# One copy and one subtraction per weight unit, and the joint tiles' low half copied by ScalarE, in the expert stage of a two-layer hybrid model

## The chip, the core and the metric

The kernel runs on one core of a Trainium2 chip. The metric is the device time of one execution in microseconds (us). The kernel before took 1473.15 us in the median of three runs (1470.57 to 1474.54).

The engines named here: TensorE (PE in the profile, its weight loads PEld), VectorE (DVE), ScalarE (ACT), GpSimd (POOL), and SyncE (SP), whose queue issues the weight transfers. Each engine takes its instructions in the order in which they stand in its queue.

## The reference

A batch of one sequence of 256 tokens, 1024 wide, goes through two layers. Layer 0 is a gated delta rule with a dense SwiGLU, layer 1 is windowed attention with a mixture of eight experts. All weights and results are float32. The part that matters here is the mixture; each expert has a hidden size of 3584:

```python
def moe_swiglu(x, w_router, w_gate, w_up, w_down):
    bsz, t, d = x.shape
    xf = x.reshape(bsz * t, d)
    logits = (xf @ w_router).astype(jnp.float32)
    top_val, top_idx = lax.top_k(logits, TOP_K)
    top_w = jax.nn.softmax(top_val, axis=-1)
    gates = jnp.einsum('nk,nke->ne', top_w, jax.nn.one_hot(top_idx, N_EXPERTS, dtype=jnp.float32))
    out = jnp.zeros_like(xf)
    for e in range(N_EXPERTS):
        h = jax.nn.silu(xf @ w_gate[e]) * (xf @ w_up[e])
        out = out + gates[:, e:e + 1].astype(xf.dtype) * (h @ w_down[e])
    return out.reshape(bsz, t, d)
```

TOP_K is 2, so an expert gets some quarter of the 256 tokens. The layer norms, the attention and the delta rule run before that, and one layer norm after it.

## The kernel before

**Weights in two parts.** TensorE works in the type fp32r, which keeps fewer bits than float32. So every weight is split: `hi` is the weight rounded to fp32r (ScalarE copies it, L154), `lo` is the rest, weight minus `hi` (VectorE subtracts, L155). Tokens are split alike. A product is then x_hi·w_hi + x_lo·w_hi + x_hi·w_lo, three matmuls.

**Units.** Weights come in units of one transfer, 128 partitions by 2048 float32 columns, 1 MB (`unit`, L140 to L156). A unit takes the next buffer of a ring of raw buffers, which SP's queue fills, and one `hi` and one `lo` buffer out of four each. A raw buffer comes free when its unit's last subtraction is done, a `hi` and a `lo` buffer when the last matmul on them is done. `quanta[0]` says in how many pieces a unit is copied and subtracted: four of 512 columns up to the third block of expert 0, then two of 1024. In the expert stage the ring has ten raw buffers; two of them are taken away for other tiles at the end of expert 6 and early in expert 7 (L1362, L1376).

**Experts.** An expert has seven blocks of 512 hidden columns. Two blocks go together, the seventh alone. A stage is a block's gate, up or down product and takes two units; an expert has 21 stages and 42 units. The loop from L1317 loads the next stage's units (L1323) ahead of this stage's matmuls. Gate goes to the PSUM banks `mm`, up to `acc`. After the up stages of a pair ScalarE applies SiLU to the gate (L1346); then the down stages of the pair before run; then follows what this text calls a hand-over (`held`, L1352 to L1358): VectorE multiplies SiLU(gate) by up (L1356), TensorE transposes the product (`turned`, L1243), ScalarE makes its `hi` (L1246) and VectorE its `lo` (L1247). An expert has four hand-overs, three of two blocks and one of one.

**Two branches.** Slots for 128 tokens are kept per expert. Where an expert has more than 64 tokens, TensorE takes the heavy branch (`heavy`, `mm3`: L170, L171, L173), 12 matmuls per unit. Where it has at most 64, it takes the light one (`mm2`, L1195), 8 matmuls per unit: a joint tile holds the `hi` of the 64 tokens in the first half of every 128 columns and their `lo` in the second, so one matmul does both token parts. The low rows are then copied (`low`, L1189) and added to the upper ones by a matmul with a folding matrix (`addlow`, L1185). The branch is TensorE's alone: ScalarE and VectorE do the same for either, joint tiles and low rows included. Expert 0 is always heavy and makes no joint tiles.

**Joint tiles.** `packed` (L1110) fills them, for the gathered tokens `xp` twice an expert (L1144), for the hidden columns `hp` once per block, seven times an expert (L1249). ScalarE copies the first half from the transposed product in PSUM (L1114), VectorE subtracts again for the second (L1115).

**Order.** The program is written stage by stage, but a scheduler orders each engine's instructions by its own costs, so where L1356, the copies and the subtractions stand relative to each other is its choice. `issue_after` (L151, L1369) holds some of them back.

Of the kernel before, what the change touches and what calls it, by code (L numbers as in the profile page):

```python
# [23 lines left out]
F32 = mybir.dt.float32  # L24
# [6 lines left out]
P = 128  # L31
# [23 lines left out]
HALF = P // 2  # L55
# [27 lines left out]
def kernel(ctx: ExitStack, tc: tile.TileContext, A, out):  # L83
    nc = tc.nc
    V, S, G, PE = nc.vector, nc.scalar, nc.gpsimd, nc.tensor
# [48 lines left out]
    quanta = [4]  # L134
# [360 lines left out]
    for tb in range(2):  # L495
        for q4 in range(2):
            p = accb()
# [25 lines left out]
    for tb in range(2):  # L523
        for q4 in range(2):
            p = accb()
# [39 lines left out]
    p = trb()  # L565
# [189 lines left out]
    with ExitStack() as fctx:  # L755
# [3 lines left out]
        hT = tuple(fp.tile([P, NF, T], F32R, name=n, bufs=1) for n in ("hTh", "hTl"))  # L759
# [237 lines left out]
    sel, gate, pos, rank = (rt.tile([P, 2, E], F32, name=n) for n in ("sel", "gate", "pos", "rank"))  # L997
# [86 lines left out]
    with ExitStack() as mctx:  # L1084
# [22 lines left out]
                        V.tensor_add(Pe[e][:, tb, :], Pe[e][:, tb, :], half[:, :P])  # L1107
            return placed

        def packed(both, p, hi):  # L1110

            v = both.rearrange("p (k l c) -> p k l c", l=2, c=HALF)
            p, hi = (t.rearrange("p (k c) -> p k c", c=P)[:, :, :HALF] for t in (p, hi))
            S.copy(v[:, :, 0], p)  # L1114
            V.tensor_sub(v[:, :, 1], p, hi.bitcast(F32))  # L1115

        def fetch(e):
            xr[e] = per.tile([P, D], F32, name="xr", tag="x0")
# [2 lines left out]
        def gather(e):  # L1121
            xg = mp.tile([P, 2, KC, P], F32R, name="xg", tag="xg")
            xp[e] = mp.tile([P, KC * P], F32R, name="xp", tag="xp") if e else None
            pg = [accb() if e == 0 else None for _ in range(2)]

            def pick(k, tb):
                PE.matmul(pg[k // 4][:, (k % 4) * P:(k % 4 + 1) * P], x[tb][:, k * P:(k + 1) * P], Pe[e][:, tb, :],
                          start=tb == 0 and k % 4 == 0, stop=tb == 1 and k % 4 == 3)

            if e == 0:  # L1130
                for k in range(KC):
                    pick(k, 0)
            for g in range(2):
                p = pg[g] if e == 0 else trb()
                for k in range(4 * g, 4 * g + 4):
                    if e == 0:
                        pick(k, 1)
                    else:
                        PE.transpose(p[:, k % 4 * P:(k % 4 + 1) * P], xr[e][:, k * P:(k + 1) * P], ident)
                hi, lo = (xg[:, n, 4 * g:4 * g + 4, :].rearrange("p a c -> p (a c)") for n in range(2))  # L1140
                S.copy(hi, p)
                V.tensor_sub(lo, p, hi.bitcast(F32))
                if e:
                    packed(xp[e][:, 512 * g:512 * (g + 1)], p, hi)  # L1144
            return xg

        xg, xp = {}, {}
# [92 lines left out]
        def turned(s, e):  # L1240
            p = trb()
            for f in range(4):
                PE.transpose(p[:, f * P:(f + 1) * P], s[:, f * P:(f + 1) * P], ident)  # L1243
            hT = mp.tile([P, 2, 512], F32R, name="hT", tag="hT")
            hp = mp.tile([P, 512], F32R, name="hp", tag="hp") if e else None
            S.copy(hT[:, 0], p)  # L1246
            V.tensor_sub(hT[:, 1], p, hT[:, 0].bitcast(F32))  # L1247
            if e:
                packed(hp, p, hT[:, 0])  # L1249
            return hT, hp  # L1250

        def keep(e):
# [57 lines left out]
        hT, held, mine, late, kept = {}, [], [], [], None  # L1310
# [6 lines left out]
        for what, e, b in stages:  # L1317
            if what != "held":
                nxt = next(nexts, None)
                if (e, b, what) == (0, 3, "gate"):  # L1320
                    quanta[0] = 2
                if nxt:
                    ready[nxt] = loads(*nxt)  # L1323
                us = ready.pop((what, e, b))
# [64 lines left out]
    with tc.If(cv > P):  # L1389
        with tc.For_i(0, E, 1) as ei, ExitStack() as octx:  # L1390
# [13 lines left out]
            for k4 in range(2):  # L1404
                p = trb()
                for kk in range(4):
                    k = 4 * k4 + kk
# [5 lines left out]
            for b in range(NB):  # L1413
                ps = []
                for n, w in enumerate((wg_, wu_)):
                    wt = op_.tile([P, KC, 512], F32, name="wt", tag="wt", bufs=2)
                    nc.sync.dma_start(wt, w[bass.ds(ei, 1)].rearrange("e (k p) n -> p (e k) n", p=P)[:, :, 512 * b:512 * (b + 1)])
                    p = mm()
# [6 lines left out]
                p = trb()  # L1425
# [63 lines left out]
```

## Time and profile before

| | |
|---|---|
| median of three runs | 1473.15 us |
| profiled execution | 1471.83 us |
| its span | 1470.1 us |
| TensorE busy | 1337.9 us (91%) |
| VectorE busy | 1202.4 us (82%) |
| ScalarE busy | 1022.4 us (70%) |
| granted TensorE clock, mean | 0.984 |
| moved over the span | 446.8 MB, 304 GB/s |

The profiled execution took 1.7 us more than its span, which runs from its first instruction to its last. A row of instructions gives engine, line, operation, what it writes and reads, the shape, the count, and behind the bar the busy time and the mean of one in ns. Behind the next bar stands how long the engine stood idle just before them and what ended that. Matmuls overlap, so a matmul's duration is longer than the time to the next one's start. A DMA share near 1 means that the sixteen transfer engines had work all the time.

### The profile page before, as it was taken

The page shows a single profiled execution, that of the slowest core. Times are in us where ns is not written, and L with a number is a line of the kernel's source. Part 1 is how long each engine was busy: PE and PEld are TensorE (multiplying, and loading weights), DVE is VectorE, ACT ScalarE, POOL GpSimd, SP SyncE. Part 2 cuts the span into 40 slices and gives each one's busy share as a digit, 9 for nine tenths or more (in the row PEclk, how much of TensorE's full clock was granted, in tenths as well). Part 3 has the DMA queues.
Part 4 walks back from the last instruction along what each step waited for, and adds up shares of the span by engine and source line. Part 5 has one row for each costly group of instructions (what it writes and reads, how often), then busy time and mean ns, then how long its engine had stood idle before and what let it go on. Part 6 is the DMA issues. An engine that isn't in the chain of part 4 may idle for free. (4 is left out here: it accounts for less than half of the span.)

```text
span 1470.1 us, 18040 instructions
## 1 busy us (share of the span) xinstructions
PE 1337.9 (91%) x6175; PEld 1041.3 (71%) x6175; DVE 1202.4 (82%) x1674; ACT 1022.4 (70%) x1519; POOL 74.5 (5%) x97
## 2 busy tenths in 40 slices
PE   7999999999998979988999999998899998888884
PEld 5888788887777868765677777765567776555552
DVE  4885965545767969899978989889998889999997
ACT  4754455443544857798887778788888778888872
POOL 4000000001000300000000000000000000001300
PEclk9999999999998989999999999999999999999997
DMA  8631587653636989999999899999999989999990
GB/s 280 199 119 59 185 287 244 227 202 84 222 115 257 381 325 371 362 392 391 390 371 365 330 353 367 354 372 378 381 391 371 367 327 385 380 377 380 418 363 30
DMA packets 145383, 446.80 MB, mean 304 GB/s; under 512 B 12704, under 2 KB 20032, under 8 KB 145264
## 3 DMA queue, kind: packets, MB, share of 16 engines
q1 hardware_dynamic: 137072, 420.64, 76.3%
q0 software_dynamic: 5280, 18.66, 3.4%
q10 hardware_dynamic: 2912, 5.90, 1.2%
q8 instruction: 76, 1.25, 0.3%
q14 instruction: 43, 0.35, 0.1%
HBM read 435.05 MB, written 15.36 MB: 306 GB/s over the span
## 5 line engine op out<-in xcount | busy, mean ns | idle before, releaser
L155 DVE TENSOR_TENSOR lo<-raw,hi 128x1024 fp32r<-128x1024 f32 (+1 forms) x928 | 930.5, 1059 | 80.2 <-ACT hi L154 76.8
L154 ACT CAST hi<-raw 128x1024 fp32r<-128x1024 f32 (+1 forms) x928 | 792.1, 927 | 147.0 <-PE acc L171 55.6
L1356 DVE TENSOR_TENSOR msg<-msg,acc 128x512 f32<-128x512 f32 x56 | 36.6, 684 | 77.1 <-ACT hi L154 38.7
L1195 PE MATMUL acc<-lo,xp 128*128 128x512 f32 x224 | 82.2, 422 | 15.8 <-DVE lo L155 14.6
L1195 PE MATMUL acc<-lo,hp 128*128 128x512 f32 x224 | 82.8, 423 | 13.9 <-DVE lo L155 12.8
L1195 PE MATMUL mm<-lo,xp 128*128 128x512 f32 x224 | 81.5, 421 | 15.3 <-DVE lo L155 14.4
L170 PE MATMUL acc<-hi,hT 128*128 128x512 f32 x224 | 89.5, 400 | 1.9 <-ACT hi L154 1.9
L171 PE MATMUL acc<-hi,hT 128*128 128x512 f32 x224 | 88.3, 394 | 0.0
L170 PE MATMUL mm<-hi,xg 128*128 128x512 f32 x224 | 87.5, 391 | 0.5 <-PEq L1179 0.5
L170 PE MATMUL acc<-hi,xg 128*128 128x512 f32 x224 | 87.9, 392 | 0.0
L171 PE MATMUL mm<-hi,xg 128*128 128x512 f32 x224 | 87.4, 390 | 0.0
L171 PE MATMUL acc<-hi,xg 128*128 128x512 f32 x224 | 87.4, 390 | 0.0
L173 PE MATMUL acc<-lo,hT 128*128 128x512 f32 x224 | 72.0, 396 | 4.1 <-DVE lo L155 4.1
L1114 ACT CAST hp<-tr 128x256 fp32r<-128x256 f32 x49 | 18.3, 374 | 81.2 <-DVE hT L1247 81.1
L1195 PE MATMUL acc<-hi,hp 128*128 128x512 f32 x224 | 71.8, 402 | 3.3 <-DVE hp L1115 3.3
L1195 PEld LDWEIGHTS acc<-lo,hp 128*128 128x128 f32 x224 | 42.5, 190 | 43.6 <-DVE lo L155 35.5
L1195 PEld LDWEIGHTS acc<-lo,xp 128*128 128x128 f32 x224 | 41.5, 191 | 44.7 <-DVE lo L155 37.9
L1195 PEld LDWEIGHTS mm<-lo,xp 128*128 128x128 f32 x224 | 41.4, 188 | 43.5 <-DVE lo L155 36.8
L1195 PE MATMUL mm<-hi,xp 128*128 128x512 f32 x224 | 68.9, 395 | 2.2 <-PEq L1179 1.5
L1195 PE MATMUL acc<-hi,xp 128*128 128x512 f32 x224 | 70.1, 400 | 0.0
L173 PE MATMUL acc<-lo,xg 128*128 128x512 f32 x224 | 68.5, 391 | 0.8 <-DVE lo L155 0.8
L173 PE MATMUL mm<-lo,xg 128*128 128x512 f32 x224 | 68.4, 391 | 0.6 <-DVE lo L155 0.6
(411 smaller groups left out, 2325.3 us busy)
## 6 DMA issues: line engine op xcount, KB each, us to landing
raw<-in_moe_w_gate_dram SPq DMA_DIRECT2D x112, 1024.0 KB, 7.0
raw<-in_moe_w_up_dram SPq DMA_DIRECT2D x112, 1024.0 KB, 7.5
raw<-in_moe_w_down_dram SPq DMA_DIRECT2D x112, 1024.0 KB, 7.4
raw<-in_a_w_in_dram SPq DMA_DIRECT2D x12, 1024.0 KB, 5.6
raw<-in_ffn_w_gate_dram SPq DMA_DIRECT2D x11, 1024.0 KB, 5.1
raw<-in_ffn_w_up_dram SPq DMA_DIRECT2D x11, 1024.0 KB, 5.1
raw<-in_ffn_w_down_dram SPq DMA_DIRECT2D x11, 1024.0 KB, 4.9
raw<-in_b_w_in_dram SPq DMA_DIRECT2D x5, 1024.0 KB, 5.0
```

Of the source, the lines that this page charges most:

```text
L154: S.copy(hi[:, c], raw[:, c])
L155: subs.append(V.tensor_sub(lo[:, c], raw[:, c], hi[:, c].bitcast(F32)))
L170: PE.matmul(ps, xh(k), wh, start=first and k == 0, stop=False)
L171: PE.matmul(ps, xl(k), wh, start=False, stop=False)
L173: PE.matmul(ps, xh(k), wl, start=False, stop=last and k == n - 1)
L1114: S.copy(v[:, :, 0], p)
L1195: PE.matmul(ps, x[:, (k0 + i % n) * P:(k0 + i % n + 1) * P], w, start=first and i == 0, stop=last and i == 2 * n - 1)
L1356: V.tensor_mul(s_, s_, pu)
```

## The change

There are three edits. `packed` gets the low part instead of the high part, and fills the second half of a joint tile with a copy on ScalarE of the low part's columns, where VectorE subtracted. The values are the same, since the low part was made by that subtraction. Both calls pass the low part. And the number of pieces per unit becomes 1 in the expert stage, except in the stages of expert 0's first two blocks, where it is 4.

```diff
-        def packed(both, p, hi):
+        def packed(both, p, lo):
 
             v = both.rearrange("p (k l c) -> p k l c", l=2, c=HALF)
-            p, hi = (t.rearrange("p (k c) -> p k c", c=P)[:, :, :HALF] for t in (p, hi))
+            p, lo = (t.rearrange("p (k c) -> p k c", c=P)[:, :, :HALF] for t in (p, lo))
             S.copy(v[:, :, 0], p)
-            V.tensor_sub(v[:, :, 1], p, hi.bitcast(F32))
+            S.copy(v[:, :, 1], lo.bitcast(F32))
...
-                    packed(xp[e][:, 512 * g:512 * (g + 1)], p, hi)
+                    packed(xp[e][:, 512 * g:512 * (g + 1)], p, lo)
...
-                packed(hp, p, hT[:, 0])
+                packed(hp, p, hT[:, 1])
...
             if what != "held":
                 nxt = next(nexts, None)
-                if (e, b, what) == (0, 3, "gate"):
-                    quanta[0] = 2
+                quanta[0] = 1 if e or b > 1 else 4
                 if nxt:
                     ready[nxt] = loads(*nxt)
```

The scheduler then orders the queues anew. Lines after L1319 have a number lower by one in the changed kernel, so L1356 is L1355 there.

VectorE's queue around the second hand-over of an expert from the third on, before. `lo<-raw,hi` is a unit's subtraction, `msg<-msg,acc` the product of gate and up, `hT<-tr,hT` the low part of its transpose, `hp<-tr,hT` the second half of the joint tile; a branch row marks where TensorE's branch stands in the program.

```order
L155 TENSOR_TENSOR lo<-raw,hi 128x1024 x2
L1179 UNCONDITIONAL_BRANCH
L155 TENSOR_TENSOR lo<-raw,hi 128x1024 x4
L1179 UNCONDITIONAL_BRANCH x2
L1356 TENSOR_TENSOR msg<-msg,acc 128x512 x2
L155 TENSOR_TENSOR lo<-raw,hi 128x1024 x5
L1179 UNCONDITIONAL_BRANCH
L155 TENSOR_TENSOR lo<-raw,hi 128x1024
L1247 TENSOR_TENSOR hT<-tr,hT 128x512
L155 TENSOR_TENSOR lo<-raw,hi 128x1024 x2
L1115 TENSOR_TENSOR hp<-tr,hT 128x4x64
```

The same place on VectorE in the changed kernel:

```order
L155 TENSOR_TENSOR lo<-raw,hi 128x2048 x2
L1179 UNCONDITIONAL_BRANCH
L155 TENSOR_TENSOR lo<-raw,hi 128x2048 x2
L1179 UNCONDITIONAL_BRANCH
L155 TENSOR_TENSOR lo<-raw,hi 128x2048
L1179 UNCONDITIONAL_BRANCH
L1355 TENSOR_TENSOR msg<-msg,acc 128x512 x2
L155 TENSOR_TENSOR lo<-raw,hi 128x2048
L1179 UNCONDITIONAL_BRANCH
L155 TENSOR_TENSOR lo<-raw,hi 128x2048
L1247 TENSOR_TENSOR hT<-tr,hT 128x512
```

Before, the product follows the last two branch marks at once, and three whole units (six halves) stand between it and the low part of the transpose. After, one whole unit stands between those two marks, ahead of the product, and two stand between the product and the low part. All four hand-overs of experts 2 to 6 are moved so, by one unit.

ScalarE's queue behind the same hand-over, before. `hi<-raw` is a unit's copy, `hT<-tr` the high part of the transpose, `hp<-tr` the first half of the joint tile.

```order
L1246 CAST hT<-tr 128x512
L154 CAST hi<-raw 128x1024 x2
L1179 UNCONDITIONAL_BRANCH
L154 CAST hi<-raw 128x1024 x2
L1114 CAST hp<-tr 128x4x64
L154 CAST hi<-raw 128x1024
L1179 UNCONDITIONAL_BRANCH
L154 CAST hi<-raw 128x1024
L1246 CAST hT<-tr 128x512
L154 CAST hi<-raw 128x1024 x2
L1114 CAST hp<-tr 128x4x64
```

And in the changed kernel, where `hp<-hT` is the new copy of the second half:

```order
L1246 CAST hT<-tr 128x512
L154 CAST hi<-raw 128x2048
L1114 CAST hp<-tr 128x4x64
L1115 CAST hp<-hT 128x4x64
L154 CAST hi<-raw 128x2048
L1179 UNCONDITIONAL_BRANCH
L1246 CAST hT<-tr 128x512
L154 CAST hi<-raw 128x2048
L1114 CAST hp<-tr 128x4x64
L1115 CAST hp<-hT 128x4x64
```

The first half's copy now comes one whole unit behind the high part, where it came two behind, and the second half follows it directly. On TensorE the transposes of the next expert's gathered tokens (L1139) are moved forward: half of them now stand between the two gate stages of the second pair, where all stood behind both. Up to the expert stage no queue has changed.

## Rows read from the trace of the kernel before

**Rows 1.** Busy time in stretches, one per expert (0 to 7), cut where ScalarE starts on an expert's first unit. Columns: the stretch, its length, then busy us and count of PE, PEld, DVE, ACT and POOL, the granted clock, the share of the transfer engines, GB/s.

```profile
443.00:597.60 154.60, 141.26 (x656) 118.55 (x655) 126.14 (x197) 101.29 (x143) 19.46 (x20) 0.92 0.89 336
597.60:713.50 115.90, 100.94 (x417) 71.80 (x415) 107.59 (x109) 100.38 (x129) 1.07 (x2) 1.00 1.00 385
713.50:839.30 125.80, 119.70 (x532) 96.16 (x533) 108.60 (x110) 100.31 (x128) 1.07 (x2) 1.00 0.94 360
839.30:966.80 127.50, 121.31 (x542) 97.60 (x540) 108.73 (x111) 100.52 (x129) 1.06 (x2) 1.00 0.92 355
966.80:1083.70 116.90, 100.27 (x398) 67.92 (x396) 108.25 (x111) 100.16 (x129) 1.07 (x2) 1.00 0.99 386
1083.70:1209.50 125.80, 119.70 (x532) 96.11 (x532) 108.62 (x110) 100.33 (x128) 1.07 (x2) 1.00 0.94 360
1209.50:1327.30 117.80, 100.55 (x396) 67.53 (x394) 109.18 (x110) 100.22 (x129) 7.70 (x5) 1.00 1.00 379
1327.30:1441.00 113.70, 96.43 (x372) 65.28 (x373) 108.25 (x114) 96.53 (x123) 17.65 (x7) 0.98 0.92 364
```

**Rows 2.** Waits in expert 4 (966.8 to 1083.7 us). Columns: engine, what and line, what ended the wait; total us, how many, the longest.

```profile
ACT hp L1114 <- DVE hT L1247: 12.3, 7, 2.9
...
DVE msg L1356 <- PE acc L1185: 8.6, 4, 3.2
...
ACT msg L1346 <- PE mm L1185: 1.8, 2, 1.1
...
ACT hT L1246 <- PE tr L1243: 1.4, 3, 1.0
```

**Rows 3.** Timeline of VectorE around the third hand-over of expert 4. Columns: start, us taken together, engine, line, operation, tiles, count, and the idle time before with what ended it.

```profile
1037.01 13.71 DVE L155 TENSOR_TENSOR lo<-raw,hi 128x1024 fp32r<-128x1024 f32 x12
1052.53 1.29 DVE L1356 TENSOR_TENSOR msg<-msg,acc 128x512 f32<-128x512 f32 x2 [1.82 <-PE acc L1185]
1053.74 6.90 DVE L155 TENSOR_TENSOR lo<-raw,hi 128x1024 fp32r<-128x1024 f32 x6
```

**Rows 4.** Timeline of TensorE at the same hand-over, the same columns.

```profile
1050.77 0.50 PE L1195 MATMUL acc<-lo,hp 128*128 128x512 f32 x1 [0.17 <-DVE lo L155]
...
1052.03 0.62 PE L1185 MATMUL acc<-low,fold 128*128 128x512 f32 x2
1053.28 1.26 PE L1243 MATMUL tr<-ident,msg 128*128 128x128 f32 x8 [0.62 <-DVE msg L1356]
```

**Rows 5.** Timeline of ScalarE at the same hand-over, the same columns.

```profile
1039.54 7.70 ACT L154 CAST hi<-raw 128x1024 fp32r<-128x1024 f32 x8
1047.92 0.60 ACT L1346 ACTIVATE msg<-mm 128x512 f32<-128x512 f32 x1 [0.67 <-PE mm L1185]
...
1049.83 3.92 ACT L154 CAST hi<-raw 128x1024 fp32r<-128x1024 f32 x4
...
1061.27 0.37 ACT L1114 CAST hp<-tr 128x256 fp32r<-128x256 f32 x1 [2.92 <-DVE hT L1247]
```

**Rows 6.** Waits from 540 to 1440 us, all those that a DMA ended.

```profile
POOL y L1366 <- DMA raw<-in_moe_w_up_dram: 75.8, 1, 75.8
...
POOL yt L1282 <- DMA ys<-yt: 8.5, 1, 8.5
...
POOL y L1367 <- DMA y<-x3d: 5.3, 1, 5.3
...
POOL yt L1282 <- DMA raw<-in_moe_w_down_dram: 0.3, 1, 0.3
```

**Rows 7.** The page's part on transfers: the up weights, KB each, median us from issue to landing.

```profile
raw<-in_moe_w_up_dram SPq DMA_DIRECT2D x112, 1024.0 KB, 7.5
```

**Rows 8.** Busy time in three stretches, the columns of rows 1.

```profile
1190.00:1330.00 140.00, 120.76 (x483) 83.28 (x482) 127.92 (x129) 117.17 (x149) 7.70 (x5) 1.00 0.98 373
1330.00:1425.00 95.00, 81.71 (x319) 55.02 (x319) 89.55 (x90) 83.33 (x106) 16.70 (x7) 1.00 1.02 405
...
1365.00:1415.00 50.00, 43.34 (x173) 29.30 (x172) 46.36 (x46) 44.83 (x56) 12.85 (x2) 1.00 1.03 417
```

**Rows 9.** Groups of instructions by line and shape. Columns: as in the section above: count, busy us, mean ns, idle us before them and what ended it.

```profile
L155 DVE TENSOR_TENSOR lo<-raw,hi 128x1024 fp32r<-128x1024 f32 x648 | 751.5, 1220 | 9.2 <-ACT hi L154 8.8
L154 ACT CAST hi<-raw 128x1024 fp32r<-128x1024 f32 x648 | 636.7, 1060 | 23.8 <-PE acc L171 13.3 <-PE mm L171 5.5 <-ACT hi L154 2.7
L155 DVE TENSOR_TENSOR lo<-raw,hi 128x512 fp32r<-128x512 f32 x280 | 179.1, 687 | 71.0 <-ACT hi L154 68.0 <-PE mm L173 2.8
...
L1246 ACT CAST hT<-tr 128x512 fp32r<-128x512 f32 x56 | 33.1, 591 | 22.0 <-PE tr L1243 22.0
...
L1115 DVE TENSOR_TENSOR hp<-tr,hT 128x256 fp32r<-128x256 f32 x49 | 20.5, 417 | 0.0
...
L1114 ACT CAST hp<-tr 128x256 fp32r<-128x256 f32 x49 | 18.3, 374 | 81.2 <-DVE hT L1247 81.1
```

**Rows 10.** Waits in expert 2 (713.5 to 839.3 us), the columns of rows 2.

```profile
DVE msg L1356 <- ACT hi L154: 12.3, 3, 5.2
...
PE tr L1243 <- DVE msg L1356: 3.8, 4, 0.9
...
DVE msg L1356 <- PEq L1179: 3.5, 1, 3.5
...
PE acc L173 <- DVE lo L155: 1.8, 4, 0.5
```

## The prediction

> **What bounds the kernel now.** I read the page first, then the table of stretches, the operations by shape, the timelines of three engines around one hand-over, the waits of two experts, and the transfers. The code that changes runs in the expert stage, so I cut that stage into its eight experts [rows 1]. The reader is to see two kinds. Experts 2, 3 and 5 issue some 530 matmuls each and TensorE is busy for 95% of them (119.7 of 125.8 us): they run the three-matmul branch, as expert 0 does, and TensorE bounds them. Experts 1, 4, 6 and 7 issue 370 to 420 and TensorE is far less full (100.3 of 116.9 us in expert 4): they run the two-matmul branch. There VectorE has 108.25 us of work in 116.9, so 8.65 us idle, and ScalarE 100.2. VectorE bounds them, and the waits say where its idle time lies: 8.6 us in four waits of L1356, the product of gate and up, for TensorE's L1185 [rows 2].
>
> The timelines show one such wait. VectorE runs twelve subtractions in a row, the last ends at 1050.72, and then L1356 stands at the head of its queue for 1.82 us [rows 3]. TensorE in that time finishes the matmuls that needed the last subtraction, adds the low rows (L1185), and transposes once L1356 has delivered [rows 4]. VectorE's queue is in order, so no later subtraction can be taken in that gap, though ScalarE was already two copies of the next units further on [rows 5].
>
> The transfers are not the bound today: between 540 and 1440 us the only waits that a DMA ended are four of POOL's [rows 6]. But they are close. Ten raw buffers at 116.9/42 = 2.78 us per unit give 27.8 us from one issue to the next into the same buffer; 7.5 us of it is the transfer [rows 7], some 6 us the copy and the subtraction, so about 14 us is reserve. And the rate is near the highest that rows show, 417 GB/s at a share of 1.03 [rows 8], which is 1.049 MB / 417 = 2.51 us per unit.
>
> **Part 1: one copy and one subtraction per unit.** A 1024-column subtraction takes 1.220 us and a 512-column one 0.687 [rows 9], so 512 columns more cost 0.533, and one of 2048 should take 1.220 + 2 x 0.533 = 2.29 us. In a row, instructions start closer together than they last: twelve took 13.71, so (13.71 - 1.22) / 11 = 1.135 from start to start [rows 3], 0.085 less than one lasts. A unit thus costs 2.27 now and 2.29 - 0.085 = 2.20 after: 0.07 saved, 2.9 us over an expert's 42 units. No row has a 2048-column subtraction. From below, 2.13 (no fixed part at all); from above 2.44 (twice 1.220, no gain and the overlap lost). I take 2.20, the line through the two rows of the same form.
>
> The Trainium skill weighs in here: VectorE: DVE Perf Modes, section "The DRAIN you can't avoid", says that the next operation does not start before the pipeline has emptied. Taken strictly, whole durations would count, 2.44 against 2.29. By that rule 0.15 us a unit and not 0.07 would go; the starts 1.135 apart speak against it.
>
> On ScalarE a 1024-column copy takes 1.060 us, eight in a row 7.70, so 0.95 from start to start [rows 5, 9]. 256 columns more cost 0.591 - 0.374 = 0.217 [rows 9], so 2048 take 1.060 + 4 x 0.217 = 1.93, or 1.82 start to start against 1.90 for two: 0.08 a unit, 3.4 us an expert. Bounds 1.74 and 2.12, by the same reasoning.
>
> **Part 2: the low half of the joint tiles.** VectorE loses nine subtractions an expert (seven for hp, two for xp), each 0.417 us [rows 9], 0.33 start to start: 3.0 us. ScalarE gains nine copies of 256 columns from SBUF. No row has that; the same shape from PSUM takes 0.374 and 512 columns take 0.591. I take 0.39, 0.28 start to start, since the shape weighs more than the source: 2.5 us. No new wait comes with it: the copy before it (L1114) already waits for the VectorE operation that writes the low half [rows 2].
>
> **Part 3: the order moves.** This is the larger term. The order of VectorE shows L1356 one unit later: in a steady expert one more whole subtraction stands before it. The 1.82 us gap then holds 2.20 us of work that is needed next anyway. Of the four waits, 8.6 us, all but the longest (3.2) vanish, and that one keeps about 1.0. L1356 itself comes up to 0.4 us later, and TensorE pays for that with time it has to spare here (16.6 us idle in expert 4).
>
> **The sum.** VectorE in expert 4: 108.25 - 2.9 - 3.0 = 102.4, plus 1.0 of the long wait, plus what it waits for ScalarE after each joint tile: two small copies and a whole one, 0.37 + 0.39 + 1.93 less three overlaps of 0.11 = 2.36, against 2.20 of work in hand, 0.16 x 7 = 1.1. That is 104.5. ScalarE: 100.2 - 3.4 + 2.5 = 99.3, plus 1.8 it waits before L1346 [rows 2], 1.4 before the copies of the transposes [rows 2], and a wait of some 0.5 at each of seven joint tiles (it copies a unit in 1.93 while VectorE must finish one in 2.20 and the 0.6 us low half): 3.5. That is 106.0, and the later of the two counts. Expert 4: 116.9 - 106.0 = 10.9 us; expert 1: 115.9 - 106.0 = 9.9.
>
> Experts 6 and 7 follow each other, and the transfers limit them, as the ring loses two buffers there too. From 1190 to 1330 us they ran at 373 GB/s, from 1330 to 1425 at 405 [rows 8]. At 417 throughout: 140 x (1 - 373/417) + 95 x (1 - 405/417) = 14.8 + 2.7 = 17.5 us. At 405 throughout: 11.1. I take 15.
>
> Experts 2, 3 and 5: four waits of TensorE for the subtraction after each hand-over, 1.8 us an expert [rows 10], go, since that subtraction is now made ahead; VectorE idled 12.3 + 3.5 us at L1356 there, enough to take it. 5.4 us in all. The rest is TensorE's own work; neither part 1 nor part 2 is felt there, and if that cover were gone, they would save rather than cost. Expert 0: nothing. Before 443 us the order of every engine is the same: nothing.
>
> 9.9 + 10.9 + 15 + 5.4 = 41 us. The profiled execution took 1471.83 us, its span 1470.1 and 1.7 around it; 1471.8 - 41 = 1431, and the median of the runs shown lies 1.3 higher: 1432 us.
>
> **Rivals.**
> - *The gap only changes its place.* VectorE takes the early subtraction, but waits just as long elsewhere, for ScalarE's copies, which now come in pieces of 1.93 us. For it: VectorE's waits for those copies are already long where pieces are small and ScalarE is not ahead (68 us before 512-column subtractions [rows 9]). Against: 8.8 us only in 648 of 1024. Left are 5.9 us in each of four experts, 23.6: 1450 us.
> - *ScalarE becomes the bound.* It keeps all its 16.7 us of waiting per light expert: 99.3 + 16.7 = 116.0, 0.9 less than now, and TensorE's experts gain nothing: 1473 - 3.6 = 1469.5 us, no change. For it: 12.3 us of those waits are for VectorE's low half, 2.9 at the longest [rows 2]. Against: these arise because ScalarE is ahead (it stood idle with two units copied [rows 5]).
> - *Slower: lockstep at the joint tiles.* L1114 waits behind VectorE's low half, which stands behind a subtraction of 2.20 rather than 1.14, and all later copies queue behind L1114. If each of nine joint tiles adds that 1.06 us to ScalarE's kept waits, a light expert takes 116.0 + 9.5 = 125.5, 8.6 more than now; four of them make 34: 1507 us. It decides once ScalarE's waits pass 116.9 - 99.3 = 17.6 us an expert. Against: the wait shrinks as ScalarE's lead does.
> - *Whole durations count.* VectorE pays each instruction's full length, so a merged pair saves 0.15. That is 3.5 us more in experts 1 and 4 and, with the transfers giving their 17.5, 10 in all: 1422 us. The rule of the Trainium skill quoted above (VectorE: DVE Perf Modes, "The DRAIN you can't avoid") would bring this; the starts of [rows 3] contradict it.
>
> **Chances.** The forecast 0.62, its own range 1418 to 1446. The gap moved 0.17; ScalarE the bound 0.08; lockstep 0.07; whole durations 0.06. A difference under 0.3% (4.4 us) cannot be told from none. Faster: 0.62 + 0.17 + 0.06 = 0.85; same 0.08; slower 0.07. The range takes in forecast, whole durations and the moved gap, with 10 us beyond the latter for a 2048-column subtraction dearer than 2.29 (at 2.44, 0.24 x 42 = 10 us in each light expert, half of it hidden where ScalarE or the transfers pace): 1412 to 1460.
>
> **What would show it.** Right: experts 1 and 4 near 106 us, with VectorE busy 102; L155 of 2048 columns at 2.29 us and L154 at 1.93; waits of L1356 for L1185 below 3 us an expert; the transfers at 410 GB/s or more from 1200 us on, and perhaps first waits of L154 for raw; experts 2, 3 and 5 at 124. Wrong: light experts still above 112; ScalarE's waits for hT grown beyond 12 us; a wait of TensorE before L1243 grown above 1 us in the heavy experts; or ScalarE waiting for transfers already in expert 4.

## The result, and the profile after

The changed kernel takes 1425.92 us in the median of four runs (1422.09 to 1427.08), against 1471.86 for the kernel before, measured beside it: a ratio of 0.968 (95% interval 0.966 to 0.971), 46 us saved. The forecast was 1432, the range 1412 to 1460. The profiled execution took 1427.08 us, its span 1425.4, at a mean granted clock of 0.982 (0.984 before).

The busy times on the page, after:

```profile
PE 1314.1 (92%) x6175; PEld 1046.2 (73%) x6175; DVE 1165.6 (82%) x1293; ACT 1012.1 (71%) x1264; POOL 68.0 (5%) x97
```

The groups by line and shape, after; columns as in [rows 9]:

```profile
L155 DVE TENSOR_TENSOR lo<-raw,hi 128x2048 fp32r<-128x2048 f32 x322 | 726.4, 2290 | 46.6 <-ACT hi L154 39.8 <-DMA raw<-in_moe_w_gate_dram 5.9
L154 ACT CAST hi<-raw 128x2048 fp32r<-128x2048 f32 x322 | 608.5, 1929 | 30.9 <-PE acc L171 18.1 <-PE mm L171 6.6 <-PE acc L173 4.6
...
L1355 DVE TENSOR_TENSOR msg<-msg,acc 128x512 f32<-128x512 f32 x56 | 36.4, 681 | 36.5 <-PEq L1179 33.3 <-PE acc L1185 2.7 <-PE acc L173 0.5
...
L1115 ACT CAST hp<-hT 128x256 fp32r<-128x256 f32 x49 | 20.6, 420 | 0.0
L1114 ACT CAST hp<-tr 128x256 fp32r<-128x256 f32 x49 | 18.6, 380 | 54.7 <-DVE hT L1247 54.7
```

A subtraction of 2048 columns takes 2.290 us and a copy 1.929, as forecast. The product now waits only 2.7 us for L1185 over the whole run; ScalarE waits 54.7 us for the low part of the transposes, where it waited 81.2 [rows 9]. But VectorE waits 39.8 us for ScalarE's copies, in 322 instructions, where it was 8.8 in 648.

VectorE at the third hand-over of expert 4, after (start, us together, the instructions, and the idle time before):

```profile
1022.50 15.50 DVE L155 TENSOR_TENSOR lo<-raw,hi 128x2048 fp32r<-128x2048 f32 x7 [0.35 <-ACT hi L154]
1037.92 1.28 DVE L1355 TENSOR_TENSOR msg<-msg,acc 128x512 f32<-128x512 f32 x2
1039.12 4.48 DVE L155 TENSOR_TENSOR lo<-raw,hi 128x2048 fp32r<-128x2048 f32 x2
```

Seven units stand in a row where there were six, and the product follows with no wait: the 1.82 us of [rows 3] are gone at this hand-over. From start to start a subtraction takes (15.50 - 2.29)/6 = 2.20 us.

For the rest I cut the time at TensorE's last hand-over transposes (L1243) of each expert, the same place in every kernel. The stretches of experts 1 to 7 after; columns as in [rows 1]:

```profile
604.70:706.10 101.40, 87.84 (x364) 63.88 (x362) 92.77 (x55) 91.19 (x89) 1.07 (x2) 0.98 1.01 390
706.10:827.10 121.00, 116.90 (x527) 95.34 (x527) 103.96 (x59) 100.83 (x95) 1.06 (x2) 1.00 1.00 388
827.10:951.40 124.30, 119.99 (x541) 97.95 (x541) 103.90 (x59) 99.85 (x94) 1.06 (x2) 1.00 0.97 364
951.40:1059.60 108.20, 96.00 (x402) 70.17 (x402) 103.14 (x59) 97.27 (x94) 1.06 (x2) 1.00 1.01 404
1059.60:1180.60 121.00, 116.86 (x527) 95.34 (x527) 103.96 (x59) 100.91 (x95) 1.07 (x2) 1.00 1.00 387
1180.60:1288.90 108.30, 95.89 (x403) 70.19 (x403) 103.20 (x59) 97.28 (x94) 1.59 (x3) 1.00 1.01 399
1288.90:1397.30 108.40, 95.14 (x381) 68.53 (x381) 106.77 (x67) 95.79 (x89) 16.39 (x9) 0.97 1.00 406
```

The same cuts in the kernels of this study, in us, each from its own trace (whole_again and after_again repeat whole_only and the changed kernel, and agree with them within 0.3 us in every expert from the first on):

| expert | before | after | whole_only | late_product | late_joint | early_whole | joint_double | pool_low |
|---|---|---|---|---|---|---|---|---|
| up to the end of 0 | 604.2 | 604.7 | 601.9 | 606.4 | 603.4 | 601.8 | 603.0 | 601.9 |
| 1, light | 102.0 | 101.4 | 101.1 | 101.3 | 100.7 | 101.1 | 104.7 | 99.7 |
| 2, heavy | 125.9 | 121.0 | 121.0 | 122.2 | 121.5 | 124.2 | 121.0 | 121.1 |
| 3, heavy | 127.4 | 124.3 | 124.3 | 124.2 | 123.7 | 128.6 | 124.4 | 124.5 |
| 4, light | 116.9 | 108.2 | 107.0 | 109.2 | 108.0 | 115.7 | 111.2 | 105.8 |
| 5, heavy | 125.8 | 121.0 | 121.0 | 122.2 | 123.2 | 126.0 | 121.0 | 121.0 |
| 6, light | 116.9 | 108.3 | 107.0 | 109.2 | 108.0 | 115.7 | 111.2 | 105.8 |
| 7, light | 119.1 | 108.4 | 108.3 | 111.9 | 110.3 | 116.9 | 110.9 | 107.8 |
| behind it | 31.8 | 28.1 | 29.7 | 30.9 | 28.3 | 33.6 | 28.2 | 31.5 |

Of the 44.7 us between the two spans, 8.7, 8.6 and 10.7 lie in experts 4, 6 and 7, 12.8 in the heavy ones, 3.7 behind the last hand-over, 0.6 in expert 1 and -0.5 before it. The cut at the start of expert 1 lies 6.6 us behind that of [rows 1] and the one at its end 7.3 us ahead, so its stretch is shorter here; by the cuts of [rows 1] it gained 2.3 us (see below).

### The profile page after: what moved, and what is told of

Its sections match the earlier page's. It is cut to its first block, busy times and chain, and to the rows that moved or that the text cites. A ratio compares the mean times of both kernels' runs of the same rounds, so it can differ in the third digit from the quotient of the medians.

```text
span 1425.4 us, 17392 instructions
## 1 busy us (share of the span) xinstructions
PE 1314.1 (92%) x6175; PEld 1046.2 (73%) x6175; DVE 1165.6 (82%) x1293; ACT 1012.1 (71%) x1264; POOL 68.0 (5%) x97
## 5 line engine op out<-in xcount | busy, mean ns | idle before, releaser
L155 DVE TENSOR_TENSOR lo<-raw,hi 128x2048 fp32r<-128x2048 f32 (+1 forms) x610 | 910.3, 1532 | 119.1 <-ACT hi L154 109.2
L154 ACT CAST hi<-raw 128x2048 fp32r<-128x2048 f32 (+1 forms) x610 | 768.4, 1310 | 156.5 <-PE acc L171 61.3
L1195 PE MATMUL acc<-lo,xp 128*128 128x512 f32 x224 | 76.8, 431 | 22.3 <-DVE lo L155 20.1
L1195 PE MATMUL mm<-lo,xp 128*128 128x512 f32 x224 | 70.8, 403 | 9.6 <-DVE lo L155 9.4
L1195 PEld LDWEIGHTS acc<-lo,xp 128*128 128x128 f32 x224 | 39.6, 195 | 50.4 <-DVE lo L155 44.5
L1195 PE MATMUL acc<-lo,hp 128*128 128x512 f32 x224 | 71.5, 400 | 3.4 <-DVE lo L155 3.4
L1195 PE MATMUL acc<-hi,hp 128*128 128x512 f32 x224 | 70.8, 397 | 1.2 <-ACT hp L1115 1.2
L1195 PE MATMUL mm<-hi,xp 128*128 128x512 f32 x224 | 68.9, 394 | 2.2 <-ACT low L1189 1.5
L1195 PE MATMUL acc<-hi,xp 128*128 128x512 f32 x224 | 70.7, 403 | 0.0
L1355 DVE TENSOR_TENSOR msg<-msg,acc 128x512 f32<-128x512 f32 x56 | 36.4, 681 | 36.5 <-PEq L1179 33.3
L1195 PEld LDWEIGHTS mm<-lo,xp 128*128 128x128 f32 x224 | 40.2, 188 | 26.8 <-DVE lo L155 19.4
L1114 ACT CAST hp<-tr 128x256 fp32r<-128x256 f32 x49 | 18.6, 380 | 54.7 <-DVE hT L1247 54.7
L1243 PE MATMUL tr<-ident,msg 128*128 128x128 f32 x224 | 34.9, 284 | 22.5 <-DVE msg L1355 22.5
```

The lines of the kernel that those rows point to most:

```text
L154: S.copy(hi[:, c], raw[:, c])
L155: subs.append(V.tensor_sub(lo[:, c], raw[:, c], hi[:, c].bitcast(F32)))
L1195: PE.matmul(ps, x[:, (k0 + i % n) * P:(k0 + i % n + 1) * P], w, start=first and i == 0, stop=last and i == 2 * n - 1)
L1355: V.tensor_mul(s_, s_, pu)
```

## Experiments

The change consists of three things: whole units (fewer, longer instructions), the joint-tile edit, and a consequence, the product standing one unit later in VectorE's queue. Two theories. **Order**: the gain comes from the product's new place, where a subtraction fills the time that VectorE stood idle. **Instruction**: it comes from fewer and longer instructions, and from the work taken off VectorE.

**whole_only.** The number of pieces alone; the joint tiles stay with VectorE. The scheduler moves the product by one unit here too.

```diff
-                if (e, b, what) == (0, 3, "gate"):
-                    quanta[0] = 2
+                quanta[0] = 1 if e or b > 1 else 4
```

> Only the pieces per unit change: one copy and one subtraction of 2048 columns; the joint tiles are still subtracted by VectorE. The scheduler puts the product one unit later here too. Order theory (the gap before the product, 8.6 us per light expert, is what is won): VectorE keeps the 3.0 us of joint subtractions per light expert, so some 12 us above the full change: 1438 us, waits of the product for the low-row matmul under 3 us in expert 4. Instruction theory (fewer and cheaper VectorE instructions win it, the gap only moves): 0.07 us x 42 units x 4 experts = 12 us below before: 1460 us.

Measured: 1423.07 us, ratio 0.966 (0.965 to 0.968), faster than either theory said, and as fast as the whole change. VectorE is busy 105.3 us in expert 4, the 2.9 us less that the prediction gave to whole units.

**joint_only.** The edits of `packed` and its two calls alone, units in halves; the product stays in its old place.

> Only the joint tiles change: ScalarE copies their low half; units stay in two pieces and the product stays where it was in VectorE's queue. Order theory: only the 3.0 us of joint subtractions per light expert go, 12 us, and the 8.6 us gap stays in expert 4: 1460 us. Instruction theory: the joint subtractions carry nearly half of 5.9 us per light expert of VectorE's time, the same 12 us and perhaps as much again from ScalarE's shorter waits: 1448 to 1460 us. Slower than 1465 would mean that ScalarE pays for the copies.

Measured: 1468.24 us, ratio 0.998 (0.996 to 0.999). In expert 4 VectorE is busy for 105.7 us instead of 108.25, yet the expert takes 117.5 us: the product still waits 8.6 us for L1185. The 2.6 us of work taken off VectorE came back as 3.1 us of waits for ScalarE (1.7 before L1142, 1.4 for the copies; none before), and the heavy experts took 1.2 to 1.7 us longer. Both theories' numbers were missed; the third case of the expectation, that ScalarE pays for the copies, is the one that came.

**early_product.** The changed kernel with the product put back to its old place, by making the next unit's subtraction wait for it (`subs` lists the subtractions in program order; a dependency inside one engine only sets the order):

```diff
-                    V.tensor_mul(s_, s_, pu)
+                    prod = V.tensor_mul(s_, s_, pu)
...
+                if e:
+                    tc.add_manual_dep(subs[-2 if b == 1 else -4].ins, prod.ins.name, mybir.DependencyInfo(
+                        mybir.DependencyClass.NoSync, mybir.DependencyReason.DATA), reason="early product")
```

> Both edits, but two added dependencies keep the product where it stood before the change, ahead of the next unit's subtraction. Order theory: the gap comes back, so expert 4 takes about 5 us more than with the full change and the heavy experts 2 us more: 4 x 5 + 3 x 2 = 26 us, 1452 us. Instruction theory: the instructions are those of the full change, so 1426 to 1430 us, with waits of the product back and other waits shorter by as much.

Measured: 1470.49 us, ratio 0.999 (0.9981 to 1.0005): nothing is left of the 46 us, where the order theory had 1452. Expert 4 takes 114.8 us with VectorE busy for 103.0. The run is not clean: expert 1 also lost 7.2 us against the kernel before, in an order that neither kernel has there, and the last product of expert 7 stands one unit earlier than in either.

**late_product.** The reverse: the kernel before, with halves and joint tiles as they were, and only the product held back by one unit. The scheduler then also placed the low part of the transpose one unit later for some blocks (three of seven in expert 4):

```diff
+                with ExitStack() as held_back:
+                    if e:
+                        held_back.enter_context(tc.issue_after(subs[-3 if b == 1 else -7].ins))
                     for bb, pu, _, s_ in mine:
-                        V.tensor_mul(s_, s_, pu)
+                        prod = V.tensor_mul(s_, s_, pu)
...
+                            for n in (2, 1) if b == 1 else (6, 5):
+                                tc.add_manual_dep(subs[-n].ins, prod.ins.name, mybir.DependencyInfo(
```

> The kernel before, instructions and all, with the product held back by one unit in VectorE's queue. Order theory: the gap of 8.6 us per light expert is filled and the heavy experts gain 1.8 us each: 4 x 7 + 5 = 33 us, 1439 us. Instruction theory: VectorE's 108 us of work per light expert is unchanged and the idle time turns up elsewhere, 1465 to 1472 us.

Measured: 1438.44 us, ratio 0.978 (0.976 to 0.980). The stretch of expert 4, columns as in [rows 1]:

```profile
954.10:1063.30 109.20, 96.62 (x402) 69.98 (x402) 108.23 (x110) 99.90 (x127) 1.07 (x2) 1.00 1.02 406
```

And in the list of its waits all that VectorE's product still waits for TensorE (L1359 is the product here):

```profile
DVE msg L1359 <- PE acc L1185: 0.5, 1, 0.5
```

VectorE does exactly the work of before (108.23 us against 108.25) in 109.2 us instead of 116.9. The gap went, 7.6 of 8.6 us. That is the order theory's number, and 33 of the 46 us.

**early_whole.** The clean form of early_product: whole_only, with the product put back from expert 2 on (the same lines, with `e > 1`). It is not the product alone here either: the low part stands one unit later for four of seven blocks of expert 4.

> whole_again (whole units, joint tiles on VectorE) with one thing changed: from expert 2 on the product of gate and up stands where it stood before, one whole unit earlier on VectorE. Theory that the order carries the gain: the waits of the product for TensorE's L1185 come back (8.6 us or more in expert 4), experts 4 and 6 take about 115 instead of 107.1, expert 7 about 116 instead of 108.4, and the heavy experts 2, 3 and 5 about 4.4 each more, since TensorE's weight loads wait for subtractions again: 1423.2 + 7.9 + 7.9 + 7.6 + 13 = 1460. Theory that whole units carry it by fewer instructions: at most 1430.

Measured: 1466.64 us, ratio 0.997 (0.995 to 0.999); 6.6 more than the order theory's 1460, of which 3.9 lie behind the last hand-over. There the added dependency puts the product one unit earlier than in any kernel without it: before and after the change the last product stands at the same place. The stretch of expert 4:

```profile
955.80:1071.50 115.70, 99.51 (x402) 69.14 (x402) 105.46 (x68) 95.17 (x85) 1.07 (x2) 1.00 0.99 383
```

Its waits of VectorE's product:

```profile
DVE msg L1355 <- PE acc L1185: 7.6, 3, 3.6
...
DVE msg L1355 <- ACT hi L154: 2.1, 1, 2.1
```

VectorE's work is that of whole_only, and 9.7 us of waits for the product are back. Whole units without the order are worth 4 to 5 us.

**late_joint.** late_product with the joint-tile edit added, so that the edit is seen beside halves in the good order.

> late_product (the kernel before with the product one unit later, halves) with the joint-tile edit added, so the edit is seen beside halves in the good order. Theory that ScalarE's extra copies pace VectorE only where ScalarE copies whole units (a copy of 1.93 us must end before the subtraction starts, against 1.06): VectorE's saving of 2.2 to 3 us per light expert is felt, experts 4 and 6 at 107, the time 1430 to 1434. Theory that the extra copies cost VectorE as much as they save whatever the piece: 1437 to 1441, as late_product's 1438.4.

Measured: 1429.15 us, ratio 0.971 (0.969 to 0.973), 9 below late_product. The intervals of the two do not touch. Of the 10.5 us between the two traces 3.0 are there before expert 0's first matmul, where the kernels are the same; 1.2, 1.2 and 1.6 lie in experts 4, 6 and 7, and 2.6 behind the last hand-over. So the edit does pay beside halves, some 6 to 7 us, and in expert 4 by half of the 2.6 us of VectorE's work that it takes off there (105.60 busy).

**after_again and whole_again**, on one chip:

> The changed kernel once more, as the measure for the three kernels beside it. If the joint-tile edit saves time beside whole units (VectorE's 2.2 us less work in a light expert are felt), it is at least 4 us faster than whole_again. If VectorE waits for ScalarE's extra copies instead, it is 2 to 5 us slower, as the first two measurements apart suggest (1425.9 against 1423.1 us).

> The kernel with the number of pieces changed alone (joint tiles filled by VectorE's subtraction, as before). Theory that the joint-tile edit costs a little: 1423 us, 2 to 5 below after_again. Theory that VectorE's busy time alone counts: 1430, some 4 x 2.2 us less 2 above it being hidden, so above after_again.

Measured: 1425.28 (1422.01 to 1425.62) against 1423.22 us (1420.68 to 1424.66); ratios 0.968 (0.966 to 0.970) and 0.967 (0.965 to 0.969). The times overlap, so that the joint-tile edit beside whole units costs anything is not shown; that it saves 4 us is excluded. The traces say why. The stretch of expert 4 in whole_again:

```profile
948.30:1055.40 107.10, 95.67 (x402) 70.25 (x403) 105.41 (x68) 94.91 (x85) 1.07 (x2) 1.00 1.01 404
```

And in after_again:

```profile
949.80:1058.10 108.30, 95.91 (x403) 70.19 (x403) 103.25 (x59) 97.31 (x94) 1.06 (x2) 1.00 1.01 404
```

The edit takes 2.2 us from VectorE, and the expert is 1.2 us longer. From the list of waits of that stretch, VectorE's for the copies, in whole_again:

```profile
DVE lo L155 <- ACT hi L154: 0.3, 1, 0.3
```

And in after_again:

```profile
DVE lo L155 <- ACT hi L154: 3.6, 9, 0.7
```

Nine waits of 0.4 us on average. In the timeline of the changed kernel five of them, 0.35 or 0.36 us each, stand at the second subtraction behind a joint tile; the other four, 0.26 to 0.66, lie where the next expert's gathered tokens come in between. ScalarE's timeline shows how one of the five comes about:

```profile
1044.24 0.37 ACT L1114 CAST hp<-tr 128x256 fp32r<-128x256 f32 x1 [2.10 <-DVE hT L1247]
1044.51 0.41 ACT L1115 CAST hp<-hT 128x256 fp32r<-128x256 f32 x1
1044.81 1.91 ACT L154 CAST hi<-raw 128x2048 fp32r<-128x2048 f32 x1
```

And VectorE's:

```profile
1044.12 2.28 DVE L155 TENSOR_TENSOR lo<-raw,hi 128x2048 fp32r<-128x2048 f32 x1
1046.76 2.29 DVE L155 TENSOR_TENSOR lo<-raw,hi 128x2048 fp32r<-128x2048 f32 x1 [0.36 <-ACT hi L154]
```

ScalarE's queue is in order too. L1114 waits for VectorE's low part; once that is there, VectorE has one subtraction in hand, and ScalarE two small copies and a whole one (to 1046.72, 2.48 us) before the next can start.

**joint_double.** The changed kernel with the second small copy made twice.

```diff
             S.copy(v[:, :, 1], lo.bitcast(F32))
+            S.copy(v[:, :, 1], lo.bitcast(F32))
```

> The changed kernel, with ScalarE's copy of the low half made twice (63 more copies of 0.42 us, some 3.4 us of ScalarE per expert; VectorE's and TensorE's work unchanged). Theory that ScalarE's copies around a joint tile pace VectorE in the light experts: VectorE's waits for ScalarE's copies grow by about 0.35 us at each joint tile of a light expert, 7 to 9 of them, so 2.5 to 3 us for experts 4 and 6, and the time is 1433 to 1438 us. Theory that ScalarE has reserve there (97 of 108 us busy): at most 1 us more, 1426 to 1428.

Measured: 1437.19 us, ratio 0.977 (0.974 to 0.979), 11.9 above after_again. Experts 1, 4, 6 and 7 take 3.2, 2.9, 2.9 and 2.5 us more, the heavy ones nothing. In expert 4 ScalarE is busy for 100.5 of 111.2 us and VectorE for 103.3, and still:

```profile
DVE lo L155 <- ACT hi L154: 6.5, 10, 0.9
```

That grew by 2.9 us (3.6 before), as much as the expert. ScalarE is idle for 10.7 us there and yet sets the pace: 6.9 us of that is waiting at L1114 for the low part, and its work on the next unit queues behind.

**pool_low.** The second small copy on GpSimd.

```diff
-            S.copy(v[:, :, 1], lo.bitcast(F32))
+            G.tensor_copy(v[:, :, 1], lo.bitcast(F32))
```

> The changed kernel, with the low half copied by GpSimd, which has almost nothing to do in the expert stage, instead of ScalarE. TensorE's order is the same, row for row. If ScalarE's copy is what costs, VectorE's waits for ScalarE fall to those of whole_again, VectorE keeps its 2.2 us saving, and the time is 1416 to 1421 us. If the transfers already pace experts 6 and 7, only experts 1 and 4 gain, 1421 to 1424. Rival: GpSimd's copy takes several us, and TensorE then waits for the joint tile in the down stage: 1430 or more.

Measured: 1422.15 us (1420.72 to 1422.94), ratio 0.966 (0.965 to 0.968). TensorE's order is the changed kernel's. Experts 4 and 6 fall to 105.8 us, 2.5 below after_again, but the stretch behind the last hand-over is 3.4 us longer. TensorE waits there 2.95 us for GpSimd's last copy, which takes 2.39 us, where it waited 1.17 us for ScalarE's in the changed kernel (more on that end below). So the rival came true at one place. The time lies in the second theory's range, but not for its reason, since expert 6 gained as much as expert 4. It is the lowest median of the study, 1.1 below whole_again, which is within what such runs scatter. From 1200 us on its transfers run at the highest rate that any row here shows (stretches, columns as in [rows 1]):

```profile
1200.00:1330.00 130.00, 115.39 (x479) 82.87 (x478) 126.98 (x72) 117.33 (x106) 31.25 (x21) 1.00 1.03 416
1330.00:1380.00 50.00, 43.28 (x174) 31.35 (x174) 49.89 (x34) 43.12 (x38) 11.39 (x5) 0.95 1.03 417
```

42 units of 1.049 MB in 105.8 us are 416 GB/s too. VectorE (103.25 us busy in expert 4's 105.7) is all but full there as well, and only one wait for a transfer is in the expert stage's trace, 0.6 us on ScalarE.

**All of it in one table** (medians in us, the kernel before at 1470.6 to 1471.8 beside each; the changed kernel is the last cell; between the rows the product's place differs, from expert 2 on in the third column and from expert 1 on in the others):

| product | halves, subtraction | halves, copy | whole, subtraction | whole, copy |
|---|---|---|---|---|
| early | 1471.8 | 1468.2 | 1466.6 | 1470.5 |
| late | 1438.4 | 1429.2 | 1423.2 | 1425.3 |

The order is worth 33 to 45 us in every column; in the last column 7.8 of the 45 are expert 1's, and in both whole columns 2 to 4 us lie behind the last hand-over, where the early kernels' product stands earlier than in any other. Without it neither edit is worth more than 5.2. With it, whole units bring 15.2, the joint edit 9.3, and both together 13.1, each with an uncertainty: in the traces late_product is 2 to 3 us behind the others before expert 0's first matmul, where nothing differs. They draw on the same few us per light expert, and then ScalarE's copies are next. That the transfers are is not shown.

## Why the prediction was right, and where it was not

**Durations.** Right. 2.29 and 1.93 us were the line through the shorter shapes, and 2.20 from start to start came out to the hundredth. The rival of whole durations falls with it: seven subtractions of 2.29 took 15.50 us, not 16.03. The sentence of the Trainium skill behind it (VectorE: DVE Perf Modes, "The DRAIN you can't avoid") thus does not hold here as taken strictly; the paragraph goes on to say that an operation that is not held starts earlier, and that is what these rows show.

**The order.** Right, and now tested both ways: late_product has it without the two cheaper forms, early_whole has whole units without it. The scheduler moved some low parts too in both, so what they test is the order around the hand-over; that the product carries it is told by its own waits, gone in one and back in the other. In expert 4 the waits of the product for L1185 fell from 8.6 to 1.3 us (forecast: 1.0 left). The rival that the gap only changes its place is excluded by late_product, where time and gap went together.

**VectorE after the joint tiles.** The mechanism was right, the size was not. The sum gave 0.16 us at seven tiles, 1.1 us; measured are 3.6 us at nine. At the tile shown above ScalarE's three copies took 2.48 us where the sum had 2.36, they began 0.12 us after the subtraction in hand, and the next one started 0.04 us after the last copy's end: 0.36 us. The two xp tiles were left out. Three times as much waiting, with 3.0 us of subtractions saved that turned out 2.2 (busy, whole_again to after_again), makes the joint edit cost 1.2 us beside whole units in expert 4, where I put it at 3.0 saved per light expert. The sum's later path was ScalarE's, 106.0 us: 99.3 of work and 6.7 of waits, 3.5 of them at L1114. Measured are 97.3 of work, and 7.2 at L1114 alone. Expert 4 gained 8.7 us, not 10.9. The rival of ScalarE as the bound is thus true in part: not by its busy time, but by what stands behind L1114.

**Heavy experts.** Forecast 1.8 each, measured 4.9, 3.1 and 4.8. The step that failed is the reading of TensorE's waits: I took them from its matmuls [rows 10]. The weight loads have waits of their own. Expert 2 before, from the list of waits:

```profile
PEld tr L1243 <- DVE msg L1356: 7.3, 8, 1.4
PEld acc L173 <- DVE lo L155: 2.6, 3, 0.9
PEld acc L1195 <- DVE lo L155: 2.0, 3, 0.9
PEld mm L173 <- DVE lo L155: 0.7, 1, 0.7
```

The waits for `lo` are 5.3 us in seven, close to the 4.9 gained; 2.0 of them, the light branch's L1195, belong to the last down stage of expert 1, which this stretch takes in. Expert 5, which also follows a light expert, has 5.3 us of them too and gained 4.8; expert 3, which follows a heavy one, has 3.0 and gained 3.1. Of expert 2 after, the same list has none of them, and all of the waits before the transposes still:

```profile
PEld tr L1243 <- DVE msg L1355: 7.3, 8, 1.4
PEld acc L1185 <- ACT low L1189: 0.6, 1, 0.6
```

The wait for a `lo` tile stands at the weight load ahead of the matmul that reads it. The matmuls of that stretch show only 2.2 us of such waits; part of the lost time is hidden in their rows, whose busy time fell from 119.2 to 116.9 us with the same work. late_product leaves 0.5 us of such waits and 122.2 us; early_whole loses 3 to 5 us in each of these experts again.

**Expert 1.** The worst step: 9.9 us forecast, 2.3 measured. In the cuts of [rows 1], which the forecast went by, its 115.9 us became 113.6:

```profile
598.10:711.70 113.60, 100.04 (x419) 74.00 (x418) 104.11 (x60) 99.14 (x96) 1.07 (x2) 0.98 1.01 391
```

I treated it as expert 4. In its stretch of the table the product's 5.1 us of waits went, and VectorE has 2.1 us less work, but its waits for ScalarE's copies grew from 0.8 to 7.0 us, one of them 3.1 long. The timeline of the changed kernel has that one at the first copy after a wait of ScalarE:

```profile
624.40 1.91 ACT L154 CAST hi<-raw 128x2048 fp32r<-128x2048 f32 x1 [3.82 <-PE acc L171]
```

And on VectorE's timeline right behind it:

```profile
626.35 2.29 DVE L155 TENSOR_TENSOR lo<-raw,hi 128x2048 fp32r<-128x2048 f32 x1 [3.09 <-ACT hi L154]
```

Expert 0 is heavy, TensorE still works on its units, and ScalarE has no free `hi` buffer until it is done with one. Before, these two waits were there too, but of 2.14 and 0.50 us. VectorE does not come to this place earlier now, so the wait grew for other reasons. One is that the subtraction now needs a whole copy of 1.91 us, where half a unit's took 1.05. The other is TensorE's clock. In both kernels TensorE stands idle for some 2 us just before, and sixteen matmuls of L1195 follow. Before, the granted clock stayed at 1.00 and they took 3.8 us; now they took 5.4, since for some of it the clock was at its lower level, 1.2 GHz:

```profile
618.00:620.00 2.00, 2.00 (x6) 1.59 (x5) 2.00 (x2) 1.31 (x1) 0.00 (x0) 0.50 1.00 363
```

Why it fell in one and not in the other is open. This is read from the traces; no run changed the number of buffers, so whether a fifth would free these 3 us is open too. That ScalarE paces the rest of this expert too is shown: joint_double lost 3.2 us in it, and pool_low gained 1.8.

**Experts 6 and 7, and the end.** Forecast 15, measured 8.6 + 10.7 = 19.3, and 3.7 behind the last hand-over that I had not counted. I had let the transfers bound both experts. Expert 6 is bounded as expert 4 is, and takes the same 108.3 us. The transfers came near the highest rate of any row here, 417 GB/s, only from 1300 us on: in the changed kernel 406 GB/s from 1190 to 1300, 416 from 1300 to 1390. That they bounded even expert 7 is not shown: VectorE is busy there for 106.8 of 108.4 us, and no engine but GpSimd waits for a transfer. The 5.9 us that the row of L155 puts to one are four waits in experts 1, 2, 3 and 5. Each ends 0.03 us after a copy of ScalarE's that had run for 1.9 us, and this copy reads the same transfer, so they are waits for the copy.

The 3.7 us at the end go with the joint edit: they are there in joint_only (28.2 against 31.8), and only 2.1 of them in whole_only. The last joint tile makes them. TensorE before, after, and in pool_low, where it begins on that tile:

```profile
1446.14 0.70 PE L1195 MATMUL acc<-hi,hp 128*128 128x512 f32 x2 [3.29 <-DVE hp L1115]
```

```profile
1402.97 0.73 PE L1195 MATMUL acc<-hi,hp 128*128 128x512 f32 x2 [1.17 <-ACT hp L1115]
```

```profile
1395.01 0.73 PE L1195 MATMUL acc<-hi,hp 128*128 128x512 f32 x2 [2.95 <-POOL hp L1115]
```

VectorE filled the second half behind two subtractions (2.35 us), ScalarE fills it at once, and GpSimd's copy takes 2.39 us. After the two longer waits the granted clock was 0.57 over the next 4 us, that is for most of them at 1.2 GHz, and two matmuls there took 1.05 us; after the shorter one it stayed at 1.00 and they took 0.62.

**The sum.** 41 forecast, 44.7 in the spans. In the cuts of [rows 1], errors of -7.6 (expert 1), -2.2 (expert 4), +7.4 (heavy), +6.3 (from expert 6 on, the end taken in) and -0.5 (before expert 1) nearly cancelled. The total was closer than its steps, and that is luck. Lockstep, the slower rival, did not come: ScalarE's waits for the low part fell in all.

## What to carry to other kernels

Where an engine with an in-order queue waits at its head while its next independent work is ready, look at what stands behind that instruction before making any instruction cheaper: one product moved by one unit was worth 33 us of 1472 here, and both cheaper forms without it some 5 at most. When work is handed from a full engine to one with idle time, ask where that idle time lies: ScalarE had some 11 us of it in each light expert, most of it at the head of the copies that VectorE then waited for. And read the waits of TensorE's weight loads beside those of its matmuls, since there the wait for a late tile was 5.3 us where the matmuls showed 2.2.

## What the runs showed of the hardware

GpSimd and VectorE hinder each other. Timelines of pool_low, GpSimd's copies first:

```profile
979.82 0.40 POOL L1115 CAST hp<-hT 128x256 fp32r<-128x256 f32 x1 [25.25 <-DVE hT L1247]
...
1038.11 2.40 POOL L1115 CAST hp<-hT 128x256 fp32r<-128x256 f32 x1 [21.62 <-DVE hT L1247]
```

and VectorE's at the third hand-over of expert 4:

```profile
1037.36 0.68 DVE L1247 TENSOR_TENSOR hT<-tr,hT 128x512 fp32r<-128x512 f32 x1
1037.96 4.68 DVE L155 TENSOR_TENSOR lo<-raw,hi 128x2048 fp32r<-128x2048 f32 x2
```

The same copy takes 0.40 us where no subtraction was running when it began, and 2.40 where one had begun 0.15 us before. The two subtractions of which the first began so, with such a copy beside them, take 4.68 us, against 4.48 in the changed kernel. So the copy waits for the subtraction (2.28 us) to end, and the next subtraction pays 0.2 us for it. The Trainium skill says this (SBUF — State Buffer, "Summary: rules for kernel authors"): of a VectorE instruction with two SBUF inputs and a GpSimd instruction that reads SBUF, the second to issue blocks until the first has finished. The trace agrees. In expert 4 seven of the nine copies took 2.39 or 2.40 us, so pool_low still pays up to 1.4 us for it there. Where VectorE had begun an instruction that reads PSUM, the trace shows the copy undisturbed. GpSimd first:

```profile
985.61 0.40 POOL L1115 CAST hp<-hT 128x256 fp32r<-128x256 f32 x1 [1.67 <-DVE hT L1247]
```

and VectorE, with `tr` in PSUM:

```profile
985.45 0.68 DVE L1142 TENSOR_TENSOR xg<-tr,xg 128x512 fp32r<-128x512 f32 x1
```

So placing GpSimd's copy beside such an instruction would save that; it was not tried.
